# A hybrid decoder layer on one core: pools of the gate tiles and of the first FFN products moved, the second norm's root with priority, the down-projection's first tiles, and 1 KB of DMA scratch

## The chip, the cores and the metric

The kernel runs on one core of a Trainium2 chip. The metric is the device time of one execution in microseconds (us). The engines are TensorE (PE in the profile), VectorE (DVE), ScalarE (ACT), GpSimd (POOL) and SyncE (SP), whose queue issues the DMAs. Each engine works its own queue in order.

## The reference

One layer (DEPTH is 1) over 1040 tokens (16 meta tokens and 1024 of the input), model width 1024, all in float32:

```python
proj = h @ w_in
q_lat, kv_lat, k_pe, z, xbc, dt_raw, g_attn, g_ssd = split(proj)
y_attn = mla_branch(q_lat, kv_lat, k_pe, ...)
y_ssd = ssd_branch(z, xbc, dt_raw, ...)   # ends in: y * silu(z), rms norm per group, * norm_g, @ w_o_ssd
mixed = sigmoid(g_attn) * y_attn + sigmoid(g_ssd) * y_ssd
h = layer_norm(ALPHA * h + mixed @ w_out)
u = causal_dwconv3(h @ w_up)              # 1024 -> 2 x 2816
gate, val = split(u, 2)
h = layer_norm(ALPHA * h + (silu(gate) * val) @ w_down)
return h[:, 16:]
```

## The kernel before, in words

Tensors lie with features on the 128 partitions and tokens along the free dimension. Each float32 product is made of three matmuls: an operand is split into a rounded high part H (a cast on ScalarE) and a rest L (a subtraction on VectorE), `split` at L197, and high by high, low by high and high by low are summed in PSUM. A split activation tile is called a form. Weights come in raw (`wraw`, two buffers), are split into `wh` and `wl` by `load_w` (L143) and are used once.

The kernel is written in Tile: the program gives operations in an order with priorities (`tc.high_priority`), and a scheduler places each instruction on its engine's queue. Tiles come from pools. A pool opened with "right" takes its place from the other end of SBUF; pools opened later reuse the place of pools that were closed, and what is written to such a place waits until the last reader of the earlier tile is done.

The stages that the change touches:

- **SSD stage** (from L767): convolutions, the scan by groups of four head pairs, and eight gate products `gs_gate` (L793). A gate has three PSUM tiles; each goes through a tanh (L801) into a tile of pool "G" (three buffers) and is stored to `ts_d` (L802). The scan's output y is stored to `y_d` (L922), the norm factors of each group to `rr_d` (L811). Four of the eight gates stand at the end of the stage.
- **y stage**: pools "Dr" (temporaries), "Dy" (33 tiles) and "Dm" on the right. `load_y` (L967) loads rr and sixteen y tiles for one half of the tokens (three buffers `yl`), multiplies (L975) and makes sixteen forms. Beside it, `w_or` is loaded in sixteen pieces and summed on VectorE (L983 to L989). Then, for each half, eight products w_o_ssd, the merge with the gates, and eight products w_out with the residual and the sum of squares (L1023 to L1040).
- **Second norm** (L1041 to L1067): `inv_root` (L201) sums over partitions with ones (L209), takes the root on VectorE and spreads it over the partitions by five matmuls (L218). `normed` (L991) scales and shifts the eight tiles (L992 on VectorE, L993 on ScalarE) and stores them to `h1_d`. Then the left-hand sides of a seven-product scheme (Strassen, Winograd's form) are formed on VectorE: T2, T3, T1, B2, and T4 after a GpSimd subtraction (L1066). The forms lie in "F1" and "F2"; the temporaries in "Dr" and "Dz".
- **FFN up-projection** (L1069 to L1215): for each of 22 blocks f, up-projection weights a11, a12 and a21, a22 are loaded; GpSimd makes s1 to s4 from them (L1106 to L1109); five splits go into pool "E1" with six buffers of each kind. Products are numbered 1 to 7; each is 24 matmuls into half a PSUM pair (`prod`). The first four blocks (`NHEAD`) are treated apart: product 1 needs only B1, which is ready since the first norm, so it stands ahead (loop at L1157), its result copied to p1 (L1164), product 2 on top, copied to c11 (L1155). Then `first(f)`, product 6, and the main loop at L1170, which ends with the stores of gate times value to `gv_d`. E1 is opened after `eD.close()`, which closes "Dr" and "Dz".
- **Down-projection** (from L1219): the residual is loaded and scaled by `load_r` (L1250) and transposed into PSUM by PE (L1291), the activations come through `load_g` (L1241), split into `dh`, the weights through `load_d` (L1226); blocks of 4, 4, 4, 5 and 5 of the 22 rows (`KBLK`, L91) are worked over four token tiles. `norm2` (L1261) needs the gains g2 and b2, which GpSimd's queue loads (L1222, L1223).

## Time and profile before

| | |
|---|---|
| runs | 2530.03, 2522.92, 2524.55 us; median 2524.55 us |
| profiled execution | 2529.95 us, span 2527.8 us, mean granted TensorE clock 0.98 |
| busy | PE 96%, DVE 66%, ACT 44%, POOL 7% of the span |
| moved | 257.10 MB, 102 GB/s in the mean; 30.9% of the 16 DMA engines' time on the hardware queue |
| chain that ended last | PE 87%, DVE 6%, DMA 2% |

The profile is one execution, and its durations are summed against its own 2529.95 us. With PE busy for 96% of the span, the questions are where the rest stands and what PE waits for there. A window gives each engine's busy time in a stretch and the granted clock as a share of full speed (2.4 GHz; 0.50 is 1.2 GHz). A timeline gives an engine's instructions in order, with the idle time ahead of each and what ended it.

### The profile page before, as it was taken

Reading aid. Unit: us, or ns where it says so; the run is one execution under the profiler, and the core shown is the slowest. Engines: PE = TensorE matmul, PEld = TensorE weight load, DVE = VectorE, ACT = ScalarE, POOL = GpSimd, SP = SyncE. Lnnn points to the kernel's source line nnn. Section 1 sums busy time; section 2 is a strip of 40 time slices with the busy share of each in tenths; the row PEclk is TensorE's granted clock in tenths of the full one; section 3 lists DMA queues with packets and bytes.
Section 4 is the critical chain, followed back from the end, with each engine's and each line's share of the span. In section 5 each row is a group of like instructions: output and inputs, shape, how many; then the busy total and the mean of one; then the engine's idle time right before and its main releaser. Section 6 shows DMA issues by size and latency. Waiting matters only on the chain.

```text
span 2527.8 us, 42547 instructions
## 1 busy us (share of the span) xinstructions
PE 2422.2 (96%) x16451; PEld 2288.7 (91%) x16451; DVE 1664.3 (66%) x3834; ACT 1112.8 (44%) x2436; POOL 167.1 (7%) x170
## 2 busy tenths in 40 slices
PE   6999999999999999999999899999599999989998
PEld 6998998899999999999999889999589999988886
DVE  6467677674557777776777376745687777765624
ACT  5335455562245554555554233422535444455211
POOL 0000000000000000000000001001332222200000
PEclk9999999999999999999999999999799999999999
DMA  5121111152432222222121375544222222247432
GB/s 200 46 65 33 37 37 34 47 156 78 155 121 90 85 70 77 85 79 82 59 94 53 117 243 167 194 132 141 84 78 89 85 77 76 76 166 233 152 103 73
DMA packets 113530, 257.10 MB, mean 102 GB/s; under 512 B 13488, under 2 KB 48560, under 8 KB 111280
## 3 DMA queue, kind: packets, MB, share of 16 engines
q1 hardware_dynamic: 113040, 253.34, 30.9%
q8 instruction: 129, 2.11, 0.3%
q0 software_dynamic: 288, 1.05, 0.1%
q14 instruction: 73, 0.60, 0.1%
HBM read 200.97 MB, written 51.26 MB: 100 GB/s over the span
## 4 chain that ended last, share of the span: by engine, by line
PE 87%; DVE 6%; DMA 2%; ACT 1%; issue 1%; POOL 0%; SPq 0%; DVEq 0%; ACTq 0%; POOLq 0%
PE d L191 25%; PE g L171 12%; PE g L173 12%; PE g L172 12%; PE c L1300 9%; PE c L605 3%; PE c L878 2%; PE c L902 1%; PE c L599 1%; PE c L882 1%; DMA yl<-y_d 1%; DVE f L199 1%; PE c L552 1%; PE c L554 1%; PE c L556 1%
## 5 line engine op out<-in xcount | busy, mean ns | idle before, releaser
L191 PE MATMUL d<-f,wh 128*128 128x258 f32 (+1 forms) x4000 | 661.5, 288 | 45.8 <-ACT p L1164 16.0
L191 PEld LDWEIGHTS d<-f,wh 128*128 128x128 f32 x4000 | 564.9, 194 | 50.3 <-ACT p L1164 16.5
L171 PE MATMUL g<-h,wh 128*128 128x348 f32 (+3 forms) x1560 | 507.0, 325 | 4.7 <-ACT lat L387 4.7
L172 PE MATMUL g<-h,wl 128*128 128x348 f32 (+3 forms) x1560 | 507.6, 325 | 0.0
L173 PE MATMUL g<-h,wh 128*128 128x348 f32 (+3 forms) x1560 | 506.6, 325 | 0.0
L191 PE MATMUL d<-f,wl 128*128 128x258 f32 (+1 forms) x2000 | 408.8, 287 | 4.0 <-DVE wl L199 2.3
L191 PEld LDWEIGHTS d<-f,wl 128*128 128x128 f32 x2000 | 317.0, 195 | 5.3 <-DVE wl L199 2.9
L161 DVE TENSOR_TENSOR wl<-wraw,wh 128x512 fp32r<-128x512 f32 (+2 forms) x278 | 194.5, 701 | 179.9 <-ACT wh L160 176.6
L171 PEld LDWEIGHTS g<-h,wh 128*128 128x128 f32 x1560 | 294.9, 189 | 7.6 <-ACT lat L387 5.0
L172 PEld LDWEIGHTS g<-h,wl 128*128 128x128 f32 x1560 | 294.9, 189 | 2.5 <-issue 2.4
L173 PEld LDWEIGHTS g<-h,wh 128*128 128x128 f32 x1560 | 294.8, 189 | 2.4 <-issue 2.4
L160 ACT CAST wh<-wraw 128x512 fp32r<-128x512 f32 (+2 forms) x278 | 167.0, 604 | 250.7 <-PE g L173 124.5
L1300 PE MATMUL c<-wh,dh 128*128 128x512 f32 x704 | 193.3, 396 | 7.7 <-ACT dh L198 7.5
L198 ACT CAST wh<-wraw 128x512 fp32r<-128x512 f32 x154 | 90.9, 619 | 246.7 <-PE c L1300 97.6
L199 DVE TENSOR_TENSOR wl<-wraw,wh 128x512 fp32r<-128x512 f32 x154 | 102.9, 693 | 133.7 <-ACT wh L198 96.5
L1300 PEld LDWEIGHTS c<-wh,dh 128*128 128x128 f32 x704 | 133.0, 190 | 38.3 <-ACT dh L198 8.1
L171 PE MATMUL g<-a,wh 128*128 128x348 f32 (+2 forms) x456 | 149.5, 328 | 1.4 <-DVE kn L199 1.1
L173 PE MATMUL g<-a,wh 128*128 128x348 f32 (+2 forms) x456 | 148.2, 325 | 0.0
L172 PE MATMUL g<-a,wl 128*128 128x348 f32 (+2 forms) x456 | 147.9, 324 | 0.0
L783 DVE SCALAR_TENSOR_TENSOR xc<-g,V,xc 128x347 f32<-128x347 f32 (+2 forms) x180 | 103.6, 575 | 41.9 <-ACT xc L779 39.0
L868 ACT ACTIVATE G<-ac,tok 116x116 f32<-116x116 f32 x288 | 91.6, 379 | 42.6 <-PE c L878 42.6
L1300 PE MATMUL c<-wl,dh 128*128 128x512 f32 x352 | 110.1, 394 | 0.0
(270 smaller groups left out, 3883.9 us busy)
## 6 DMA issues: line engine op xcount, KB each, us to landing
wraw<-win SPq DMA_DIRECT2D x65, 512.0 KB, 3.4
wraw<-wup SPq DMA_DIRECT2D x48, 512.0 KB, 3.6
wraw<-wdl SPq DMA_DIRECT2D x44, 512.0 KB, 3.6
ac<-cs_d SPq DMA_DIRECT2D x16, 1044.0 KB, 5.6
wraw<-wos SPq DMA_DIRECT2D x32, 512.0 KB, 4.0
gv<-gv_d SPq DMA_DIRECT2D x44, 256.0 KB, 4.1
yl<-y_d SPq DMA_DIRECT2D x32, 257.0 KB, 3.8
wraw<-wout SPq DMA_DIRECT2D x16, 512.0 KB, 3.4
```

Source lines behind the costliest of these rows:

```text
L160: nc.scalar.copy(h[:, :n * ncol], r)
L161: nc.vector.tensor_sub(l[:, :n * ncol], r, f32(h[:, :n * ncol]))
L171: nc.tensor.matmul(ps, ah, bh, start=(k == 0), stop=False)
L172: nc.tensor.matmul(ps, al, bh, start=False, stop=False)
L173: nc.tensor.matmul(ps, ah, bl, start=False, stop=(k == n - 1))
L191: nc.tensor.matmul(ps[:, PO + c0:PO + c1], a, b[:, c0:c1], start=(start and k == 0 and i == 0), stop=(k == n - 1 and i == 2), skip_group_c ...
L198: nc.scalar.copy(H, src)
L199: nc.vector.tensor_sub(L, src, f32(H))
L605: nc.tensor.matmul(ops[:, o0:n], vt[j][:w, hh * P:(hh + 1) * P], ptt[:w, o0:n], start=(j == 0), stop=(j == nbmax - 1))
L783: nc.vector.scalar_tensor_tensor(t[:, l:n], ps[:, hal + l - s:hal + n - s], vec("cw", (3 - s) * 24 + ct), t[:, l:n], ALU.mult, ALU.add)
L868: nc.scalar.activation(G_[:, k * S:(k + 1) * S], ac[:S, hh, C0[b] + k * S:C0[b] + (k + 1) * S], AF.Relu, bias=tok[:, 3 * b + k, 32 + hd:33 ...
L1300: nc.tensor.matmul(pss[q], a, b, start=False, stop=(k == NFF - 1 and i == 2))
```

## The change

1. Pool "G" is opened on the left below "py", ahead of the o_proj stage, and closed after it; the right side is free during the SSD stage.
2. A pool "E0" is opened beside "F2", ahead of the second norm. It holds p1, c11, s1 to s4, and the splits for products 7, 6 and 3 (four buffers). "E1" comes after the first four blocks' products 1 and 2, and holds the splits for 5 and 4 (three buffers), u2, u4, ga, va and gb. The four b21 tiles are temporaries in "Dr" now, loaded late.
3. The second norm's `inv_root` has priority 400, the loop over the first four blocks 300 instead of 200. GpSimd's order is s1, s2, s3, s4. The condition that starts a block ahead has f + 1 instead of f + 2.
4. In the down-projection the blocks are 2, 4, 4, 4, 4, 4; `dh` of the first four rows has a pool of its own with 8 tiles; g2 and b2 go through SyncE's queue, and are placed after `norm2`.
5. The DMA scratch of the program is 1 KB.

```diff
-KBLK = ((0, 4), (4, 8), (8, 12), (12, 17), (17, 22))
+KBLK = ((0, 2), (2, 6), (6, 10), (10, 14), (14, 18), (18, 22))
...
     cut_psum(3)
+    eG = ctx.enter_context(ExitStack())
+    pgs = eG.enter_context(pool("G", 3))
     eY = ctx.enter_context(ExitStack())
     pyy = eY.enter_context(pool("py", 48))
...
-    with pool("G", 3, "right") as pgs, pool("C", 1) as p:
+    with pool("C", 1) as p:
...
     eY.close()
+    eG.close()
...
     eM.close()
     pf2 = eF.enter_context(pool("F2", 40))
-    pz = eD.enter_context(pool("Dz", 8, "right"))
-    rd = inv_root(ssq, HN, 1.0 / D, LN_EPS)
+    p0 = eF.enter_context(pool("E0", 1))
+    pz = eD.enter_context(pool("Dz", hB, "right"))
+    with tc.high_priority(400):
+        rd = inv_root(ssq, HN, 1.0 / D, LN_EPS)
...
-    b11, b21 = [], []
+    b11 = []
     for j in range(hB):
-        for b, k in ((b11, j), (b21, j + hB)):
-            b.append(ftile(pz, F32))
-            nc.sync.dma_start(b[-1], h1_d[k][:, cols(0)])
+        b11.append(ftile(pz, F32))
+        nc.sync.dma_start(b11[-1], h1_d[j][:, cols(0)])
...
     for j in range(hB):
-        nc.gpsimd.tensor_sub(b21[j], b21[j], t2[j])
-        T4[j] = form(pf2, b21[j])
-    eD.close()
-    pe = eF.enter_context(pool("E1", 1))
+        b21 = dtmp("b21", "r", 8)
+        nc.sync.dma_start(b21, h1_d[j + hB][:, cols(0)])
+        nc.gpsimd.tensor_sub(b21, b21, t2[j])
+        T4[j] = form(pf2, b21)
...
-            def stile(name):
-                return pe.tile([P, 512], F32, name=name, tag=name)
-
-            s1, s2, s3, s4 = (stile(k) for k in ("s1", "s2", "s3", "s4"))
-            nc.gpsimd.tensor_sub(s3, a11, a21)
+            s1, s2, s3, s4 = (p0.tile([P, 512], F32, name=k, tag=k) for k in ("s1", "s2", "s3", "s4"))
             nc.gpsimd.tensor_add(s1, a21, a22)
             nc.gpsimd.tensor_sub(s2, s1, a11)
+            nc.gpsimd.tensor_sub(s3, a11, a21)
             nc.gpsimd.tensor_sub(s4, a12, s2)
...
             for q, a in ((4, a22), (7, s3), (6, s2), (5, s1), (3, s4)):
-                r[q] = wsplit(pe, a, 6)
+                r[q] = wsplit(p0, a, 4) if q in (7, 6, 3) else wsplit(pe[0], a, 3)
...
-    def etile(name, bufs, n=HN):
-        return pe.tile([P, n], F32, name=name, tag=name, bufs=bufs)
+    pe = []
+
+    def etile(name, bufs):
+
+        return (p0 if name in ("p1", "c11") else pe[0]).tile([P, HN], F32, name=name, tag=name, bufs=bufs)
...
-        st[f]["c11"] = etile("ga", NHEAD + 1)
+        st[f]["c11"] = etile("c11", NHEAD)
...
-        with tc.high_priority(200):
+        with tc.high_priority(300):
...
+    eD.close()
+    pe.append(eF.enter_context(pool("E1", 1)))
     first(0)
...
-        ga = conv_up(c11, f, "ga", NHEAD + 1)
+        ga = conv_up(c11, f, "ga", 2)
...
-        while begun < min(NFF, f + (3 if f + 2 < NHEAD else 2)):
+        while begun < min(NFF, f + (3 if f + 1 < NHEAD else 2)):
...
-    with pool("Er", 8) as pr, pool("Eh", 50) as ph, pool("Ew", 1) as p:
-        g2 = p.tile([P, D], F32, name="g2")
-        b2 = p.tile([P, D], F32, name="b2")
-        nc.gpsimd.dma_start(g2, ln2[0:1].broadcast_to([P, D]))
-        nc.gpsimd.dma_start(b2, ln2[1:2].broadcast_to([P, D]))
+    with pool("Er", 8) as pr, pool("Eh0", 8) as ph0, pool("Eh", 44) as ph, pool("Ew", 1) as p:
...
-                H = ph.tile([P, 512], F32R, name="dh", tag="dh")
-                L = ph.tile([P, 512], F32R, name="dh", tag="dh")
+                H, L = ((ph0 if k < 4 else ph).tile([P, 512], F32R, name="dh", tag="dh") for _ in range(2))
...
+        g2 = p.tile([P, D], F32, name="g2")
+        b2 = p.tile([P, D], F32, name="b2")
+        nc.sync.dma_start(g2, ln2[0:1].broadcast_to([P, D]))
+        nc.sync.dma_start(b2, ln2[1:2].broadcast_to([P, D]))
         for r in range(2):
...
-    nc = _bacc.Bacc("TRN2", target_bir_lowering=False, num_devices=1)
+    nc = _bacc.Bacc("TRN2", target_bir_lowering=False, num_devices=1, dynamic_dma_scratch_size=1024)
```

The change moves instructions on several engines. In the rows below, the lines of the changed kernel are some three higher than before (L977 is the load of yl, L974 that of rr, L804 the store of a gate tile, L1168 the copy to p1, L1159 that to c11, L996 the norm's shift). A number behind a name tells tiles apart.

SyncE's queue at the end of the gates, before: the last gate's stores, then the first loads of rr and y.

```order
L802 DMA ts_d7_143<-ga_16884 128x334
L802 DMA ts_d7_143<-ga_16912 128x348
L802 DMA ts_d7_143<-ga_16940 128x344
L147 DMA wraw_17272<-wos 128x1024
L971 DMA rr_16963<-rr_d0_160 128x514
L974 DMA yl_16965<-y_d0_144 128x514
L974 DMA yl_16972<-y_d1_145 128x514
L974 DMA yl_16979<-y_d2_146 128x514
```

The same place in the changed kernel, at the stores of gate 5:

```order
L977 DMA yl_16986<-y_d3_147 128x514
L977 DMA yl_16995<-y_d4_148 128x514
L804 DMA ts_d5_141<-ga_16696 128x334
L977 DMA yl_17002<-y_d5_149 128x514
L974 DMA rr_17053<-rr_d3_163 128x514
L804 DMA ts_d5_141<-ga_16724 128x348
L977 DMA yl_17009<-y_d6_150 128x514
L977 DMA yl_17016<-y_d7_151 128x514
L977 DMA yl_17025<-y_d8_152 128x514
L804 DMA ts_d5_141<-ga_16752 128x344
L147 DMA wraw_17145<-wos 128x1024
L977 DMA yl_17032<-y_d9_153 128x514
```

The loads of y3 to y15 stand between the gate stores now; those of y0 to y2 stand in the SSD stage, and the sixteen loads of `wor` in the stage before.

PE at the second norm, before (d_20630 and d_20667 are product 1 of blocks 0 and 1):

```order
L209 MATMUL d_20448<-ones_74,ssq_19905 128x1 x5
L218 MATMUL d_20469<-K_73,ir_20455 128x128
L191 MATMUL d_20630<-f_18953,wh_20622 128x258
L191 MATMUL d_20667<-f_18953,wh_20659 128x258
L191 MATMUL d_20630<-f_18953,wh_20622 128x256
L191 MATMUL d_20667<-f_18953,wh_20659 128x256
```

and in the changed kernel (there d_20628 and d_20665):

```order
L209 MATMUL d_20451<-ones_74,ssq_19905 128x1 x5
L218 MATMUL d_20472<-K_73,ir_20458 128x128 x2
L218 MATMUL d_20472<-K_73,ir_20458 128x2
L218 MATMUL d_20472<-K_73,ir_20458 128x128 x2
L191 MATMUL d_20628<-f_18953,wh_20620 128x258
L191 MATMUL d_20665<-f_18953,wh_20657 128x258
L191 MATMUL d_20628<-f_18953,wh_20620 128x256
L191 MATMUL d_20665<-f_18953,wh_20657 128x256
```

Before, the other four L218 stand behind the 48 matmuls of these two products; now all five stand ahead of them.

ScalarE at the forms and the copies to p1, before (f_20596 to f_20611 are T4's):

```order
L198 CAST f_20596<-f_20477 128x514
L198 CAST f_20601<-f_20481 128x514
L198 CAST f_20606<-f_20485 128x514
L198 CAST f_20611<-f_20489 128x514
L198 CAST wh_20884<-wraw_20874 128x512
L1164 COPY p1_20655<-d_20630 128x514
L198 CAST wh_20888<-s3_20878 128x512
L198 CAST wh_20892<-s2_20877 128x512
L198 CAST wh_20896<-s1_20876 128x512
L198 CAST wh_20900<-s4_20879 128x512
L1164 COPY p1_20692<-d_20667 128x514
```

and in the changed kernel, first among the norm's shifts, then at the splits for products 7, 6 and 3 of block 0:

```order
L198 CAST f_20495<-t2_20493 128x514
L996 ACTIVATE r_20098<-r_20098,V_72 128x514
L198 CAST wh_20720<-wraw_20718 128x512
L198 CAST wh_20724<-wraw_20718 128x512
L1168 COPY p1_20653<-d_20628 128x514
L1168 COPY p1_20690<-d_20665 128x514
L198 CAST f_20508<-t2_20506 128x514
L996 ACTIVATE r_20366<-r_20366,V_72 128x514
L198 CAST f_20521<-t2_20519 128x514
L198 CAST wh_20783<-wraw_20781 128x512
L1168 COPY p1_20753<-d_20728 128x514
```

```order
L198 CAST wh_20891<-s3_20881 128x512
L198 CAST wh_20895<-s2_20880 128x512
L198 CAST wh_20903<-s4_20882 128x512
L1159 COPY c11_20716<-d_20628 128x514
L1159 COPY c11_20779<-d_20665 128x514
L1159 COPY c11_20842<-d_20728 128x514
L1159 COPY c11_20868<-d_20791 128x514
L198 CAST f_20574<-r_20232 128x514
L198 CAST f_20578<-r_20299 128x514
L198 CAST f_20582<-r_20366 128x514
```

The copies to p1 stood behind the last form; now three of them stand among the norm's shifts, and the copies to c11 stand behind the split of s4, ahead of the casts of B2 and T4.

## Rows read from the trace of the kernel before

**Rows 1.** The page: busy time, and PE by forty slices.
```profile
PE 2422.2 (96%) x16451; PEld 2288.7 (91%) x16451; DVE 1664.3 (66%) x3834; ACT 1112.8 (44%) x2436; POOL 167.1 (7%) x170
...
PE   6999999999999999999999899999599999989998
```

**Rows 2.** Windows; columns: stretch, length, each engine's busy time (count), clock, DMA, GB/s.
```profile
1443.90:1500.00 56.10, 42.62 (x290) 40.27 (x290) 42.51 (x68) 18.23 (x31) 0.00 (x0) 0.85 0.84 268
1500.00:1510.00 10.00, 10.00 (x85) 10.00 (x84) 4.56 (x7) 3.12 (x5) 0.00 (x0) 1.00 0.60 194
690.00:720.00 30.00, 30.00 (x192) 29.80 (x192) 10.60 (x21) 6.45 (x13) 0.24 (x3) 1.00 0.41 131
```

**Rows 3.** PE timeline, gates to w_o_ssd; columns: start, busy, engine, line, what [idle before].
```profile
1443.60 0.32 PE L173 MATMUL g<-h,wh 128*128 128x344 f32 x1
1453.06 0.80 PE L191 MATMUL d<-f,wh 128*128 128x258 f32 x2 [9.14 <-ACT f L198]
```

**Rows 4.** SyncE timeline, same place: DMA issues.
```profile
1425.64 8.38 SPq L802 DMA_DIRECT2D ts_d<-ga  x3
...
1436.90 8.38 SPq L802 DMA_DIRECT2D ts_d<-ga  x3
...
1445.85 0.39 SPq L971 DMA_DIRECT2D rr<-rr_d  x1
```

**Rows 5.** Windows, second norm to FFN, and the FFN loop.
```profile
1754.96:1900.00 145.04, 106.66 (x774) 104.33 (x774) 103.84 (x150) 62.38 (x102) 41.08 (x28) 0.84 0.25 80
1900.00:2200.00 300.00, 300.00 (x2488) 300.00 (x2487) 222.69 (x298) 144.70 (x237) 80.67 (x60) 1.00 0.25 78
```

**Rows 6.** PE timeline, 1750 to 1800.
```profile
1757.23 1.25 PE L209 MATMUL d<-ones,ssq 128*128 128x1 f32 x10 [2.27 <-DVE ssq L1039]
1760.90 0.76 PE L218 MATMUL d<-K,ir 128*128 128x128 f32 x2 [2.42 <-DVE ir L230]
...
1769.31 1.05 PE L218 MATMUL d<-K,ir 128*128 128x128 f32 x8
...
1783.36 0.77 PE L191 MATMUL d<-f,wh 128*128 128x258 f32 x2 [9.62 <-ACT r L993]
...
1799.46 0.80 PE L191 MATMUL d<-f,wh 128*128 128x258 f32 x2 [11.54 <-ACT p L1164]
```

**Rows 7.** ScalarE timeline, forms and p1.
```profile
1794.27 2.18 ACT L198 CAST f<-f 128x514 fp32r<-128x514 f32 x4
...
1798.82 0.58 ACT L1164 COPY p<-d 128x514 f32<-128x514 f32 x1
```

**Rows 8.** PE timeline, start of the down-projection.
```profile
2269.06 2.07 PE L1300 MATMUL c<-wh,dh 128*128 128x512 f32 x4 [7.54 <-ACT dh L198]
```

**Rows 9.** ScalarE timeline, same place.
```profile
2267.19 1.26 ACT L1257 ACTIVATE hr<-hr 128x512 f32<-128x512 f32 x2 [0.37 <-DMA hr<-h_d]
```

**Rows 10.** Groups on DVE, 1450 to 1500: line, what, shapes, count | busy, mean | idle before.
```profile
L975 DVE SCALAR_TENSOR_TENSOR yl<-yl,half_sg,rr 128x514 f32<-128x514 f32 x16 | 11.8, 752 | 9.6 <-DMA yl<-y_d 9.5
L199 DVE TENSOR_TENSOR f<-yl,f 128x514 fp32r<-128x514 f32 x16 | 11.0, 687 | 0.2
L987 DVE TENSOR_REDUCE wm<-wr 128x1 f32<-128x512 f32 x16 | 10.6, 678 | 0.0
```

**Rows 11.** DVE timeline, second norm.
```profile
1771.30 2.06 DVE L992 SCALAR_TENSOR_TENSOR r<-r,V,d 128x514 f32<-128x514 f32 x3
...
1781.82 1.40 DVE L992 SCALAR_TENSOR_TENSOR r<-r,V,d 128x514 f32<-128x514 f32 x2
...
1785.60 2.39 DVE L1059 TENSOR_TENSOR r<-r 128x514 f32<-128x514 f32 x2
```

**Rows 12.** The page's DMA issues: count, KB each, median us to landing.
```profile
wraw<-wup SPq DMA_DIRECT2D x48, 512.0 KB, 3.6
```

**Rows 13.** GpSimd timeline, second norm.
```profile
1785.81 1.63 POOL L1066 TENSOR_TENSOR f<-f,t 128x514 f32<-128x514 f32 x1 [2.50 <-issue]
1798.95 2.26 POOL L1106 TENSOR_TENSOR s<-wraw 128x512 f32<-128x512 f32 x1 [11.51 <-DVE f L199]
```

## The prediction

> **What bounds the kernel now.** The page comes first: TensorE (PE) is busy 96% of the 2527.8 us span, and its row of forty slices falls below 9 only at the start, in a few slices in the middle and at the end [rows 1]. So only time in which PE stands still, or runs at half clock, can be won. I then looked for the stretches where it does, with the windows, and read in each the PE timeline for the wait and the queue of the engine named as releaser. Three such stretches lie where the diff works.
>
> **Stretch A, from the last gate product to the first products of w_o_ssd (1443.9 to 1500).** 290 matmuls ran in 56.1 us; the ten us behind show the full rate, 85 in 10 us [rows 2]. At that rate 290 take 34.1 us, so 22.0 us are lost. The timeline shows the largest piece: the last gate matmul ends at 1443.92, the next starts at 1453.06 after 9.14 us, released by ScalarE's cast of a form [rows 3]; the rest is smaller waits and the lower clock behind that wait (0.85 granted over the whole stretch [rows 2]). The cause stands in SyncE's queue: the loads of rr and yl are issued at 1445.85 and not before, behind the stores of the last three gate tiles [rows 4]. Those y tiles lie on the right side of SBUF where the gate tiles "G" stood.
>
> **Stretch B, from the second norm into the first FFN products (1754.96 to 1900).** 774 matmuls in 145.04 us; the 300 us behind ran 2488 in 300 us, 0.1206 us each [rows 5]. 774 of them are 93.3 us: 51.7 us lost. The PE timeline names the pieces [rows 6]: 2.27 and 2.42 us around the root; the other four broadcasts of the root (L218) at 1769.31, 8 us after the first, behind 48 matmuls; 9.62 us released by L993 of the norm; 11.54 us released by the copy to p1 (L1164), and smaller ones. That copy needs a tile of pool E1, which opens only when Dz, Dr and their tiles are closed, that is, after the T4 forms: the copy runs at 1798.82, right behind the last casts of forms [rows 7].
>
> **Stretch C, into the down-projection.** PE waits 7.54 us before 2269.06 for the first cast of dh [rows 8], which stands on ScalarE right behind two scalings of hr that end at 2268.45 [rows 9].
>
> **The change, part by part: A.** With "G" on the left the y stage's right-hand tiles wait for nothing of the gates. By the order, the loads of y0 to y2 go into the SSD stage, y3 to y15 between the last nine gate stores, and the sixteen sums of w_or go back into the o_proj and gate stage, where DVE is busy 10.60 of 30 us [rows 2]: the 16 by 0.678 us = 10.8 us [rows 10] are hidden there. Thirteen forms remain to be made during the gates. One costs DVE 0.752 + 0.687 us [rows 10], 18.7 us in all, against nine gate tiles at a third of the 11.26 us from the stores of one gate to those of the next (1425.64 to 1436.90 [rows 4]), about 34 us. If they were late by two or three us it would still cost nothing, since the first product takes the sixteen forms one after another over 96 matmuls, 11.3 us. What is left is the tanh that frees the last gate's PSUM, about 1.1 us (estimate: a cast that stands ahead of it and itself, each near a cast's 0.55 us [rows 7]). The new place has a price: SyncE now waits in the SSD stage for stores of y and rr to land, six or seven times, with weight loads queued behind it. The raw weights are two buffers ahead, and PE was never short there; I take 0 and keep 5 us as the bad end. **A: 22.0 - 1.1 = 20.9 us gained, bounds 15 and 22.**
>
> **B.** The root with priority puts all five L218 together, so the norm starts when the first two did, some 8 us earlier (1761.7 instead of 1770.4 [rows 6]). Pool E0 holds p1, c11 and s1 to s4 beside F2 from the start, so the p1 copies wait for no form. The second products (x0 with q 2) and f3's first then run during the norm. What still is lost, on the clock of before:
> - ssq, root and broadcasts, unchanged: 1754.96 to 1760.90 less little work, 5.9 us.
> - f3's first product takes the PSUM pair that rd holds, so it waits for the eighth L992. Before, these took from 1771.30 to 1783.22 [rows 11], 11.9 us; from 1763.2, and with four weight splits and p1 copies put between, that is 1776.9. PE has 72 matmuls until then, to about 1773: 4 us.
> - The seconds last until about 1789.6. f0's product 6 then waits for c11, which stands on ScalarE behind the split of s4. Its raw load can be issued when f3's low half is split, about 1782.5, lands 3.6 us later [rows 12], five POOL instructions of 1.3 us end at 1793.0, two ScalarE ones at 1794.3: 4.7 us.
> - Product 5 needs the split of s1, which stands behind three c11 copies, eight casts of forms (four took 2.18 us [rows 7]) and another split: about 1803.3 against 1798.4 for PE: 5 us.
> - f1's and f2's splits of s2 come late by 3 and 1.5 us.
> - PE starts at half clock after each longer wait, four times. Such a start took 8.0 us for 48 matmuls between 1761.31 and 1769.31 [rows 6], against 5.8: 2.2 us, so 8.8 in all.
>
> Together 5.9 + 4 + 4.7 + 5 + 4.5 + 8.8 = 32.9 us. **B: 51.7 - 32.9 = 18.8 us gained.** The bounds: if every wait is 50% longer and the clock falls once more, 8 us; if the queues overlap as well as they can and only the root, f3's wait and two half-clock starts stay (14 to 20 us), 32 us. I take the value in the middle, since each step has its own row.
>
> **C.** The 1 MB of g2 and b2 leaves the time of the first gv loads, and one hr scaling fewer stands between the last store and dh; the gv loads still stand behind the same stores. Lower bound 0; upper 3 us, somewhat under half of the 7.54. I take 1.5, about one scaling (0.63) and a landing shorter by one us. The smaller first block needs only two gv tiles for its first 48 matmuls, which hid nothing before: PE showed no wait after 2269.06. The scratch size only makes room.
>
> **Nothing.** The loop from f = 4 on ran without a gap, 300.00 of 300 us [rows 5]. Its five splits had six buffers of each kind and now have four and three, which is one to spare in each pool; by the order each split stands at least 140 matmuls, some 17 us, ahead of its product. I cost it at 0; the cover is that distance.
>
> **Sum.** 20.9 + 18.8 + 1.5 = 41.2 us. The profiled execution took 2529.95 us and would take 2488.8. The median of the runs shown is 2524.55, 5.4 lower; taking the same 41 us off gives **2483.5 us**.
>
> **The rivals.**
> 1. *VectorE and GpSimd hold each other up.* Beside a GpSimd subtraction of 1.63 us [rows 13] two VectorE subtractions took 2.39 us, where two instructions of the same size just before took 1.40 [rows 11]. After the change four more GpSimd instructions (s1 to s4 of f0) fall among the forms, and each would add its length to VectorE's chain: 4 by 1.3 to 1.6 us, some 6 us, passed on to the waits for s1 and for f1's weights. GpSimd in turn would wait for VectorE: the first sum that ran beside a form took 2.26 us [rows 13]. With both B gains 10, the total is 32: 2492. For: the rows. Against: part of it is already in the forms' times. Chance 0.15.
>    The Trainium skill, "SBUF — State Buffer", section "SBUF: two separate sides", says that the port pair of the two engines is an exclusive lock, held for the whole instruction, against a VectorE operation with two inputs in SBUF. By that rule the forms' subtractions would be blocked in full, and the trace agrees in the pair of rows just named.
> 2. *B's waits only move.* The chain raw load, GpSimd, ScalarE for f0 to f2 is late by as much as the p1 copies were, so B gains 4: 26 us in all, 2498. For: GpSimd still starts its sums only after the raw load. Against: some 96 matmuls more are done by then. Chance 0.12.
> 3. *B hides nearly all*, 30 us: 52 us, 2472. For: three of the waits reckoned above hang on ScalarE's in-order queue, where one that ends earlier lets all behind it pass. Chance 0.11.
> 4. *Slower: the narrow weight pools in the loop.* If a split in E1 (three buffers) waits for its slot until the product of the f before is done, PE stalls once in each of the 18 iterations from f = 4. At 2.3 us each (cast, subtraction and a wait between engines: 0.6 + 0.7 + about 1) that is 41 us and eats the gain; slower than before by over 0.3% takes 2.7 us each, at 3.5 us it would be 2546. Against: the 17 us of distance. Chance 0.04.
> 5. *It doesn't do what it says*: the scheduled order shows the moves, so only if waits at run time hold them back to the same end. Within 0.3%. Chance 0.03.
>
> **How the numbers follow.** My own case has 0.55. It lies between 2477 and 2490. The range takes the bounds of A, B and C: 15 + 8 + 0 = 23 gives 2501.5, 22 + 32 + 3 = 57 gives 2467.5; so 2467 to 2502, which holds rivals 1 to 3 and leaves out 4 and 5 and the odd miss beyond the bounds. About 0.3%, 7.6 us, is what a measurement can tell from no change. Faster by more: 0.55 + 0.15 + 0.12 + 0.11 = 0.93, of which I move 0.01 to no change for what I have not seen: 0.92; within: 0.04; slower: 0.04.
>
> **What would show it.** A right: no wait over 2 us on PE between the gates and w_o_ssd, yl loads among the gate stores on SyncE, clock 1.00 there. B right: L218 five times in one row, p1 copies among the norm's instructions, then two waits of about 5 us near c11 and the split of s1. C right: a wait of about 6 instead of 7.5 us before the first down-projection matmul. Wrong, if PE has gaps between 1900 and 2200 of the old clock, if the SSD stage is longer by over 5 us, or if the second norm's stretch still loses over 45 us.

## The result and the profile after

The changed kernel takes 2496.43 us (median of 4 runs, 2494.66 to 2499.16) against 2524.91 us (4 runs, 2522.92 to 2530.03): 28.5 us less, a ratio of 0.9885 with a 95% interval from 0.9868 to 0.9902. The forecast was 2483.5 us in a range from 2467 to 2502: the right side and inside the range, but 13 us better than what came.

Where the time went is read by cutting the span at five points of the PE timeline: the end of the last gate matmul, of the last w_out matmul, of the last FFN product, the start of the first down-projection matmul and the end. Each stretch is the difference of two such times.

| kernel | A: gates to second norm | B: second norm and FFN products | C: to the down-projection | D: down-projection |
|---|---|---|---|---|
| before | 311.0 | 501.3 | 12.8 | 258.7 |
| changed | 294.0 | 490.5 | 12.2 | 260.4 |
| e1: G on the left alone | 291.5 | 500.5 | 12.6 | 258.3 |
| e2: changed, G on the right | 307.5 | 488.5 | 11.4 | 259.1 |
| e3: root's priority alone | 311.2 | 495.7 | 12.5 | 259.0 |
| e4: changed, old blocks | 295.5 | 488.9 | 12.0 | 258.1 |
| e5: changed, b21 on VectorE | 291.8 | 488.0 | 11.4 | 259.3 |
| e6: changed, product 4's split in E0 | 291.7 | 514.9 | 10.8 | 259.6 |
| e7: changed, c11 first | 294.1 | 489.0 | 12.6 | 258.0 |
| e8: changed, y15's cast on VectorE | 290.9 | 489.5 | 12.1 | 262.0 |
| e9: changed, no priority for the root | 294.3 | 495.4 | 10.9 | 260.9 |
| e10: changed, no forms of B2 and T4 | 295.8 | 483.8 | 12.1 | 259.3 |
| e11: b21 and y15 on VectorE | 290.0 | 485.9 | 12.5 | 259.9 |
| e12: e10 with three raw buffers | 292.3 | 479.9 | 11.4 | 258.3 |

Each row is one profiled execution, and unchanged code differs by 1 to 4 us between rows, so a difference of one or two in one cell says nothing by itself: with the changed kernel's code there, A is 291.7 to 295.8 and B 488.5 to 490.5. Before against changed, A gives 17.0, B 10.8, C 0.6 and D -1.6; the remaining 3.8 of the 30.6 us between the two spans lie ahead of A. They can't be put down to the change: the gates end at 1439 to 1444 in all these runs, at 1443.9 before and at 1440.7 in e3, which has the old code there.

The page of the changed kernel, the same two lines as before [rows 1]:

```profile
PE 2412.9 (97%) x16451; PEld 2279.8 (91%) x16451; DVE 1675.0 (67%) x3834; ACT 1111.7 (45%) x2436; POOL 168.5 (7%) x168
...
PE   6999999999999999999999999999789999989998
```

The dip at the gates is gone, that at the second norm is shallower (a 5 before, now a 7 and an 8). The PE timeline, at the four places of [rows 3, 6, 8]:

```profile
1443.28 0.50 PE L191 MATMUL d<-f,wh 128*128 128x258 f32 x2 [3.11 <-ACT ga L803]
...
1736.47 1.25 PE L209 MATMUL d<-ones,ssq 128*128 128x1 f32 x10 [2.27 <-DVE ssq L1042]
1740.15 2.47 PE L218 MATMUL d<-K,ir 128*128 128x128 f32 x10 [2.43 <-DVE ir L230]
...
1774.58 0.80 PE L191 MATMUL d<-f,wh 128*128 128x258 f32 x2 [5.78 <-ACT c L1159]
...
1783.10 0.77 PE L191 MATMUL d<-f,wh 128*128 128x258 f32 x2 [3.19 <-DVE u L1147]
...
2236.82 2.07 PE L1305 MATMUL c<-wh,dh 128*128 128x512 f32 x4 [8.45 <-ACT dh L198]
```

The 9.14 us behind the gates became 3.11. The five L218 stand in one row (ten records, 2.47 us). The waits for L993 and for p1, 9.62 and 11.54 us, are gone; in their place stand 5.78 us for c11 and 3.19 us. The down-projection waits as before: 8.45 us here, 7.54 in the kernel before, 7.08 to 8.88 in the other runs. The windows of the changed kernel (columns as in [rows 2, 5]):

```profile
1440.17:1500.00 59.83, 56.72 (x470) 56.73 (x471) 23.73 (x35) 16.70 (x28) 0.00 (x0) 1.00 0.44 145
...
1734.20:1742.27 8.07, 3.37 (x21) 3.35 (x21) 3.98 (x15) 1.25 (x2) 0.00 (x0) 0.77 0.22 65
1742.27:1750.33 8.06, 7.42 (x51) 7.22 (x50) 7.10 (x12) 4.69 (x8) 0.00 (x0) 0.80 0.45 166
1750.33:1768.80 18.47, 17.97 (x144) 17.54 (x144) 15.56 (x25) 11.57 (x21) 4.34 (x3) 1.00 0.46 157
1768.80:1774.58 5.78, 0.00 (x1) 0.01 (x1) 3.13 (x3) 2.40 (x5) 5.78 (x6) 0.84 0.03 9
1774.58:1790.08 15.50, 11.19 (x49) 10.42 (x49) 11.60 (x18) 10.93 (x19) 5.91 (x6) 0.62 0.19 65
1790.08:1854.52 64.44, 54.10 (x416) 52.24 (x417) 52.30 (x67) 25.64 (x41) 20.95 (x15) 0.97 0.26 87
1854.52:1880.00 25.48, 25.42 (x196) 25.21 (x197) 21.65 (x26) 11.22 (x18) 10.54 (x8) 0.93 0.22 73
1880.00:2180.00 300.00, 300.00 (x2487) 300.00 (x2485) 229.75 (x298) 145.77 (x237) 78.67 (x58) 1.00 0.25 80
```

From 1880 on PE is full again at 2487 matmuls in 300 us. Taking 0.1206 us per matmul off the stretches ahead of that gives what each lost: 8.1 for the root (its small matmuls counted as lost), 1.9 for the start at a granted 0.80, 1.1, 5.8, 9.6 at a granted 0.62, 14.3 between 1790 and 1854, and 1.8.

The same can be counted in both kernels, since PE runs the same number of these matmuls in every run: 192 of the first four blocks' products 1 and 2, then as many as block 0 has left (120), as blocks 1 to 3 have (360) and as block 4 has (168). They are counted in order of time, so a product of the next block that runs early is counted with the block ahead. These are the windows of the 360 before and in the changed kernel (two of the 362 matmuls reach in from ahead):

```profile
1835.27:1890.27 55.00, 48.71 (x362) 47.71 (x361) 44.25 (x59) 20.23 (x32) 17.11 (x12) 0.91 0.27 87
```

```profile
1800.66:1858.02 57.36, 48.27 (x362) 46.83 (x361) 48.58 (x62) 23.85 (x37) 18.21 (x13) 0.94 0.26 84
```

At 0.1206 us each, 360 matmuls take 43.4 us. What each part of B lost, counted in this way:

| lost, us | before | changed | e5 | e10 | e12 |
|---|---|---|---|---|---|
| root, to the first product | 6.4 | 8.1 | 8.1 | 8.1 | 8.1 |
| the 192, and the wait behind them | 34.3 | 9.2 | 6.2 | 7.3 | 6.8 |
| block 0's 120 | 2.0 | 11.6 | 11.6 | 9.3 | 9.3 |
| the 360 of blocks 1 to 3 | 11.6 | 13.9 | 14.3 | 10.1 | 8.6 |
| block 4's 168 | 0.0 | 0.4 | 0.8 | 1.9 | 0.0 |

In e2, e4 and e8, whose code in B is the changed kernel's, the second line is 8.3 to 9.0, the third 11.4 to 12.0 and the fourth 11.4 to 13.5. So of the 25 us won at the 192 block 0 gives ten back, and blocks 1 to 3 lose at least what they lost before, within the scatter of these runs.

### The profile page after: what moved, and what is told of

Read it like the earlier page. It is cut to its first block, busy times and chain, and to the rows that moved or that the text cites. A ratio compares the mean times of both kernels' runs of the same rounds, so it can differ in the third digit from the quotient of the medians.

```text
span 2497.2 us, 42526 instructions
## 1 busy us (share of the span) xinstructions
PE 2412.9 (97%) x16451; PEld 2279.8 (91%) x16451; DVE 1675.0 (67%) x3834; ACT 1111.7 (45%) x2436; POOL 168.5 (7%) x168
## 4 chain that ended last, share of the span: by engine, by line
PE 83%; DVE 7%; DMA 4%; ACT 2%; issue 1%; POOL 1%; SPq 0%; DVEq 0%; ACTq 0%; POOLq 0%
PE d L191 24%; PE g L171 12%; PE g L173 12%; PE g L172 12%; PE c L1305 7%; PE c L605 3%; PE c L880 2%; PE c L904 1%; PE c L599 1%; PE c L884 1%; DMA yl<-y_d 1%; DMA gv<-gv_d 1%; DVE f L199 1%; PE c L552 1%; PE c L554 1%
## 5 line engine op out<-in xcount | busy, mean ns | idle before, releaser
L172 PEld LDWEIGHTS g<-h,wl 128*128 128x128 f32 x1560 | 294.3, 189 | 2.5 <-issue 2.4
L199 DVE TENSOR_TENSOR wl<-wraw,wh 128x512 fp32r<-128x512 f32 x154 | 111.5, 750 | 150.6 <-ACT wh L198 106.6
```

The costliest lines, as they stand in the source:

```text
L172: nc.tensor.matmul(ps, al, bh, start=False, stop=False)
L199: nc.vector.tensor_sub(L, src, f32(H))
```

## The experiments

A ratio in brackets, with its 95% interval, is to the kernel before, timed anew beside each group of runs; its median there was 2523.66 to 2525.30 us. Differences to the changed kernel are to its 2496.43 us, from another group, so one or two us of such a difference say little.

### e1, e2: the gate tiles' pool

The pools of the o_proj stage need the place of the larger scratch once G stands on the left, so the two go together (the runs don't take them apart, but e2 keeps the scratch), and e1 is the kernel before with

```diff
+    eG = ctx.enter_context(ExitStack())
+    pgs = eG.enter_context(pool("G", 3))
     eY = ctx.enter_context(ExitStack())
-    with pool("G", 3, "right") as pgs, pool("C", 1) as p:
+    with pool("C", 1) as p:
+    eG.close()
-        nc.gpsimd.dma_start(g2, ln2[0:1].broadcast_to([P, D]))
+        nc.sync.dma_start(g2, ln2[0:1].broadcast_to([P, D]))
...
+    ..., dynamic_dma_scratch_size=1024)
```

and e2 the changed kernel with the pool's lines undone (the scratch and the loads of g2 and b2 kept).

> The kernel before with pool G on the left, the 1 KB scratch (without which the pools of the o_proj stage don't fit) and, since the scratch belongs to GpSimd's DMAs, g2 and b2 loaded by SyncE at their old place. Theory (the parts add up): the changed kernel's trace shows 17 us less between the last gate product and the second norm, so 2524.9 - 17 = 2508 us, and the second norm's stretch loses its 51.7 us as before. Rival (the y loads only displace other waits, which come back later in the stretch or in the SSD stage): 2515 us or more.

> The changed kernel with pool G back on the right. Theory: the 17 us come back, 2496.4 + 17 = 2513 us, the 9 us of PE idle time before w_o_ssd stand in the trace again. Rival (other parts of the change cover some of it): 2505 us or less.

e1 took 2507.91 us, 17.0 less than before (ratio 0.9934, 0.9918 to 0.9951); e2 took 2514.31, 17.9 more than the changed kernel (0.9956 against before, 0.9939 to 0.9973). The first wait of PE behind the gates in each (PE timeline):

```profile
1445.67 0.51 PE L191 MATMUL d<-f,wh 128*128 128x258 f32 x2 [2.58 <-ACT ga L803]
```

```profile
1449.39 0.80 PE L191 MATMUL d<-f,wh 128*128 128x258 f32 x2 [9.13 <-ACT f L198]
```

The place of G makes the 9 us wait, and nothing else in the change covers it. The waits on stores that came into the SSD stage cost nothing that shows: e1's gates end at 1443.1, those of before at 1443.9, and those of e3, with the old order, at 1440.7.

### e3, e9: the root's priority

e3 is the kernel before with the priority alone; e9 the changed kernel without it.

```diff
-    rd = inv_root(ssq, HN, 1.0 / D, LN_EPS)
+    with tc.high_priority(400):
+        rd = inv_root(ssq, HN, 1.0 / D, LN_EPS)
```

> The kernel before with the priority on the second norm's root and nothing else: the five L218 stand together, p1 still waits for the T4 forms. Theory (the priority carries most of the gain at the second norm, because the forms and so the p1 copies end some 8 us earlier): 2524.9 - 8 = 2517 us. Rival (pool E0 carries it: without it the first GpSimd sums, the weights' split and the p1 copies wait for something else than the forms): within 3 us of before, 2522 to 2525.

> The changed kernel without the priority on the second norm's root, so that four of the five L218 stand behind the products 1 of blocks 0 and 1 again. The priority alone took 5.6 us off the stretch from the second norm to the end of the FFN products in the kernel before, all parts together 10.8. Theory (the two add up): the stretch loses 5 to 6 us, 2501.5 to 2502.5 us. Rival (with E0 the p1 copies don't hang on the forms, so the later forms are hidden): 2499 or less.

e3: 2518.68 us, 6.2 less than before (0.9977, 0.9966 to 0.9988). e9: 2503.37 us, 6.9 more than the changed kernel (0.9907, 0.9892 to 0.9922). Both are within 2 us of their theories and away from their rivals. B is 5.6 us shorter in e3, 4.9 longer in e9. e3's PE timeline and ScalarE's copy to p1 in it:

```profile
1758.48 2.47 PE L218 MATMUL d<-K,ir 128*128 128x128 f32 x10 [2.42 <-DVE ir L230]
...
1791.44 0.80 PE L191 MATMUL d<-f,wh 128*128 128x258 f32 x2 [11.69 <-ACT p L1165]
```

```profile
1790.81 0.58 ACT L1165 COPY p<-d 128x514 f32<-128x514 f32 x1
```

The p1 wait is as long as before (11.69 against 11.54), but the whole chain of forms ends earlier: the copy starts at 1790.81 instead of 1798.82, of which 3.0 us come from the earlier start of the stretch and 5.0 from the priority. That is less than the 8 us between the first and the later L218 of before, in part since all five take 2.47 us here. So the two parts add up: about 5 us of B belong to the priority, about 5 to the rest of the change there, that is, E0 with the new orders and the loop's priority, which no run takes apart.

### e4: the blocks of the down-projection

```diff
-KBLK = ((0, 2), (2, 6), (6, 10), (10, 14), (14, 18), (18, 22))
+KBLK = ((0, 4), (4, 8), (8, 12), (12, 17), (17, 22))
```

> The changed kernel with the old blocks of the down-projection (4, 4, 4, 5, 5). From the first down-projection matmul to the end the changed kernel took 260.4 us where the kernel before took 258.7, with a new wait of 0.95 us on a weight split and a lower clock behind it. Theory (the new blocks put casts of dh that wait for gv loads ahead of that split): the wait goes, 1 to 2 us less, 2494.5 to 2495.5, with 258.7 in the trace. Rival (g2 and b2 on SyncE's queue hold the weight loads up): the wait stays, 2496.

2496.77 us, as the changed kernel: the rival's time. The wait did go, as the theory had it: behind its first wait PE has none in D, where the changed kernel has 0.95 us at 2297.99; of the ten profiles with the new blocks six have such a wait (0.73 to 1.57 us), of the four with the old ones none. But D is 258.1 here, and e7, which has the new blocks, has 258.0, e8 262.0. Over all profiles the new blocks have 258.0 to 262.0 and the old ones 258.1 to 259.0: 1.2 us on average against the new blocks (259.7 of ten, 258.5 of four), too little for the times to show.

### e5: GpSimd beside VectorE

```diff
-        nc.gpsimd.tensor_sub(b21, b21, t2[j])
+        nc.vector.tensor_sub(b21, b21, t2[j])
```

> The changed kernel with the four b21 subtractions on VectorE instead of GpSimd. In the changed kernel's trace GpSimd's first sum takes 3.11 us beside a run of form subtractions, one b21 stands between s2 and s4 (1.72 us), and product 6 waits 5.78 us for c11 behind the split of s4. Theory (the price of the two engines beside each other is a few tenths of each instruction, and only the b21 ahead of s4 counts): s4 ends 1.5 us earlier, VectorE gets 2.8 us more work, in sum -2 to +1 us: 2494.5 to 2497.5. Rival 1 of the prediction (GpSimd and VectorE holding each other up is what the missing 8 us of the second norm's stretch went to): 4 us or more less, 2492 or below.

2493.01 us (0.9871, 0.9854 to 0.9887): 3.4 less than the changed kernel, between the two expectations. B is 2.4 less than in the changed kernel and 0.5 to 1.5 less than in e2, e4 and e8; e11, with the same edit here, has 485.9. GpSimd's first sums in the changed kernel and here:

```profile
1764.46 3.11 POOL L1107 TENSOR_TENSOR s<-wraw 128x512 f32<-128x512 f32 x1 [45.58 <-DMA wraw<-wup]
1767.53 1.29 POOL L1109 TENSOR_TENSOR s<-wraw 128x512 f32<-128x512 f32 x1
1768.78 1.26 POOL L1108 TENSOR_TENSOR s<-s,wraw 128x512 f32<-128x512 f32 x1
1770.00 1.72 POOL L1072 TENSOR_TENSOR b<-b,t 128x514 f32<-128x514 f32 x1
1771.68 1.70 POOL L1110 TENSOR_TENSOR s<-wraw,s 128x512 f32<-128x512 f32 x1
```

```profile
1761.68 1.44 POOL L1107 TENSOR_TENSOR s<-wraw 128x512 f32<-128x512 f32 x1 [45.18 <-DMA wraw<-wup]
1763.08 1.75 POOL L1109 TENSOR_TENSOR s<-wraw 128x512 f32<-128x512 f32 x1
1764.80 1.73 POOL L1108 TENSOR_TENSOR s<-s,wraw 128x512 f32<-128x512 f32 x1
1766.61 1.59 POOL L1110 TENSOR_TENSOR s<-wraw,s 128x512 f32<-128x512 f32 x1
```

From the start of the first sum to the start of s4 it was 7.22 us and is 4.93: one b21 less (1.72); the first sum is 1.67 shorter, but the next two are 0.93 longer together. PE's wait for c11 went from 5.78 to 3.22, and the one behind it from 3.19 to 3.91; blocks 1 to 3 lose as much as in the changed kernel (14.3 and 13.9). The shorter first sum isn't the edit's doing: e4, whose code here is the changed kernel's, has 1.48, 1.74 and 1.74 for the three, and a wait of 4.91 for c11. So what the edit surely saves is b21's place in GpSimd's queue. The two engines' mutual delay remains in e5, and no run shows what it costs alone.

### e6: which split lies in which pool

```diff
-            for q, a in ((4, a22), (7, s3), (6, s2), (5, s1), (3, s4)):
-                r[q] = wsplit(p0, a, 4) if q in (7, 6, 3) else wsplit(pe[0], a, 3)
+            for q, a in ((7, s3), (6, s2), (4, a22), (5, s1), (3, s4)):
+                r[q] = wsplit(p0, a, 4) if q in (7, 6, 4) else wsplit(pe[0], a, 3)
```

> The changed kernel with the split for product 4 (of the raw half a22) in E0 and that for product 3 in E1, so that a22 is split ahead of the forms of B2 and T4. Theory (the missing 8 us stand in blocks 1 to 3: their second raw load waits for the buffer that a22 of the block before holds, and that split waits for its place in E1, which is free only behind the last forms; the load was issued at 1783.58 where the first stood at 1773.41): block 1's second load is issued some 8 us earlier, the small waits of blocks 1 to 3, some 11 us of idle time and low clock, fall by half: 2496.4 - 5 = 2491.5 us. Rival (these waits come from GpSimd's four sums per block and ScalarE's queue, whatever the load does): within 2 us, 2494.5 to 2498.

2523.80 us (0.9993, 0.9982 to 1.0004): both expectations missed, by 26 us or more. The load did move: block 1's two raw loads are issued at 1773.38 together (SyncE's timeline, against 1773.41 and 1783.58 in the changed kernel). But the loop, which had no gap, now has small ones, 11.7 us in 300 (windows, and ScalarE's waits from 1900 to 2200, in e6 and then in the changed kernel: what waited for what, us in total, times, longest):

```profile
1900.00:2200.00 300.00, 288.33 (x2324) 283.58 (x2325) 199.38 (x276) 132.15 (x221) 82.33 (x56) 0.99 0.21 73
```

```profile
ACT wh L198 <- DMA wraw<-wup: 96.6, 14, 8.1
```

```profile
ACT wh L198 <- DMA wraw<-wup: 41.8, 14, 4.0
```

ScalarE's queue waits 96.6 us of 300 for loads instead of 41.8, with the copies that free PSUM behind it, and 2324 matmuls run where 2487 did. B is 24.4 us longer, 1.4 us for each of 18 blocks: this is the fourth rival of the prediction in a version two lines away. The likely reason is that product 4 is a block's last: with its split in the pool of four a raw half stays in its buffer longer, and the next load comes later. But the edit changes the order of the splits together with their pools, so which of the two did it is not shown.

### e7: c11 ahead of the splits

```diff
-        nc.scalar.copy(st[f]["c11"], half(st[f]["x0"]))
+        with tc.high_priority(600):
+            nc.scalar.copy(st[f]["c11"], half(st[f]["x0"]))
```

> The changed kernel with a higher priority for the copies to c11, which puts three of them ahead of the splits of s2 and s4 on ScalarE. Theory (PE's 5.78 us before product 6 are half ScalarE's order: c11 is copied only behind the split of s4, 3.3 us after that of s2): product 6 then starts behind the split of s2, the wait is 2.5 to 3 us shorter, and of this 1 to 3 us reach the end: 2493.5 to 2495.5. Rival (the next wait, for product 5, takes it all back, since it hangs on the casts of the forms): 2496 to 2497.5.

2498.41 us (2495.80 to 2501.82): no gain, and B, at 489.0, is that of e2, e4 and e8. In the PE timeline the 5.78 us fall apart, and the next wait grows:

```profile
1769.75 0.50 PE L191 MATMUL d<-f,wh 128*128 128x258 f32 x2 [1.35 <-ACT wh L198]
1772.73 0.79 PE L191 MATMUL d<-f,wl 128*128 128x258 f32 x2 [2.48 <-DVE wl L199]
...
1782.14 0.77 PE L191 MATMUL d<-f,wh 128*128 128x258 f32 x2 [4.33 <-DVE u L1147]
```

1.35 and 2.48 us for the split of s2, then 4.33 where there were 3.19: product 5 takes most of it back, as the rival said.

### e8: the last tanh

```diff
+                if hi == 0 and ti == 15:
+                    H, L = ftile(pyh), ftile(pyh)
+                    nc.vector.tensor_copy(H, yt)
+                    nc.vector.tensor_sub(L, yt, f32(H))
...
```

> The changed kernel with the cast of the last y form (y15, first half) on VectorE instead of ScalarE. In the changed kernel's trace PE waits 2.3 to 3.6 us behind the last gate product for the last tanh, where the prediction had 1.1, and on ScalarE that tanh and the one before stand behind the cast of y15, whose load landed last. Theory (ScalarE's order makes it): the wait falls to 1 to 1.5 us, 2494 to 2496 us. Rival (the tanh waits for its tile, that is, for the store of an earlier gate tile on SyncE): the wait stays over 2 us, 2496 to 2497.

2497.02 us (2493.50 to 2499.08), no difference in the times; the trace answers. ScalarE at the last gate of the changed kernel, and PE's first wait in e8:

```profile
1440.86 0.62 ACT L198 CAST f<-yl 128x514 fp32r<-128x514 f32 x1 [3.29 <-DVE yl L978]
1441.39 0.45 ACT L803 ACTIVATE ga<-g 128x348 f32<-128x348 f32 x1
...
1442.77 0.46 ACT L803 ACTIVATE ga<-g 128x344 f32<-128x344 f32 x1
```

```profile
1443.81 0.50 PE L191 MATMUL d<-f,wh 128*128 128x258 f32 x2 [1.07 <-ACT ga L803]
```

In the changed kernel a tanh of gate 7 waited behind the cast of y15 (3.29 us for VectorE's product, that is, for the load), and the last one behind that and two casts of a weight. Without the cast the wait is the 1.07 us of the prediction, and 1.07 again in e11, which has the same edit; in all the other runs with G on the left it is 2.10 to 3.57. A is 3.1 us shorter in e8 and 4.0 in e11, where unchanged code differs by 4; in e8 D is 1.6 longer than in the changed kernel.

### e10, e12: the late forms and the raw buffers

e10 leaves work out, so its result is not the layer's:

```diff
-    for j in range(hB):
-        B2[j] = form(pf2, rs[j + hB])
-    for j in range(hB):
-        b21 = dtmp("b21", "r", 8)
-        nc.sync.dma_start(b21, h1_d[j + hB][:, cols(0)])
-        nc.gpsimd.tensor_sub(b21, b21, t2[j])
-        T4[j] = form(pf2, b21)
+    B2, T4 = T1, T2
```

> The changed kernel without the forms of B2 and T4 (their products read T1's and T2's forms instead, so that eight casts, eight subtractions and the four b21 loads and subtractions are left out). Theory (the missing 8 us of the second norm's stretch hang on these forms: E1's place is free only behind them, so the splits for products 5 and 4 of block 0 come late, with them the raw buffer and the load of block 1): product 5's wait goes (3 us and the low clock behind it), block 1's second load is issued some 8 us earlier, and the stretch loses 6 to 9 us less: 2487.5 to 2490.5 us. Rival (GpSimd's sums and two raw buffers bound blocks 1 to 3 whatever the forms do): 2 to 4 us less, as without the b21 subtractions on GpSimd, 2492.5 to 2494.5.

2489.72 us (2488.66 to 2491.99), 6.7 less than the changed kernel; B is 6.7 less, and 4.7 to 5.7 less than in e2, e4 and e8, whose code in B is the changed kernel's. Of it some 2.4 are the b21 subtractions (e5), so the forms of B2 and T4 hold PE up by some 2 to 4 us; whether by their casts or by their subtractions no run tells. PE's waits and block 1's raw loads (SyncE):

```profile
1773.54 0.80 PE L191 MATMUL d<-f,wh 128*128 128x258 f32 x2 [4.12 <-ACT c L1153]
...
1782.99 1.22 PE L191 MATMUL d<-f,wh 128*128 128x258 f32 x4 [5.00 <-ACT wh L198]
```

```profile
1772.38 1.48 SPq L1085 DMA_DIRECT2D wraw<-wup  x2
```

The loads go out together, as forecast, but product 5's wait didn't go: 5.00 us, for the next thing in line. e12 adds a third raw buffer (`bufs=3` at the three places of `wraw`), in the place of the sixteen form tiles:

> As the kernel without the late forms (eight casts, eight subtractions, the b21 loads and subtractions left out), with a third buffer for raw weights, which the place of the sixteen form tiles makes room for. There PE still waits 5.00 us before product 5 of block 0 and 6 us in six small waits in blocks 1 to 3. Theory (two raw buffers bound these blocks: each block needs two loads, and the second waits until a half of the block before is split): the stretch from the second norm to the end of the FFN products loses 3 to 5 us less, 479 to 481 us of 483.8, and the whole 2485 to 2487 us. Rival (one set of s1 to s4 and ScalarE's queue bound them): the stretch stays within 1.5 us, the whole 2488 to 2491 us.

2487.66 us (2484.34 to 2491.34); the median is 2.1 below e10, and the ranges overlap. B is 479.9, 3.9 less, as the theory had it (the whole lies 0.7 above its range), but the profile of e12 is of its fastest execution and that of e10 of its slowest, so 3.9 may be too much. GpSimd's sums of blocks 0 and 1 in e12:

```profile
1753.83 1.29 POOL L1102 TENSOR_TENSOR s<-wraw 128x512 f32<-128x512 f32 x1 [40.85 <-DMA wraw<-wup]
...
1776.36 1.66 POOL L1102 TENSOR_TENSOR s<-wraw 128x512 f32<-128x512 f32 x1 [7.22 <-DVE wl L200]
```

Block 0's sums start 11.2 us earlier than in e10 (1753.83 against 1765.00; 2.2 of it come from the earlier start of the stretch), since the raw load no longer waits for a buffer. The next bound shows at once: block 1's s1 waits 7.22 us for the split of block 0's s1, of which there is one tile. A second set of s tiles wasn't tried, so that this is what holds blocks 1 to 3 now is not shown.

### e11: a version that beats both

> The changed kernel with the b21 subtractions and the cast of y15 on VectorE, as the version that may beat both kernels. Theory (the two act in different stretches and add up): 2493.0 less 1 to 2 us, 2491 to 2492 us. Rival (the second is hidden by the first products' waits on weights): 2493.

With both edits, e5's and e8's: 2491.92 us (2489.02 to 2492.81; 0.9873, 0.9858 to 0.9887), 31.7 less than the kernel before beside it (2523.66) and 4.5 less than the changed kernel (2494.66 to 2499.16); 1.1 less than e5 alone, as much as the expectation and less than the scatter.

## Why the prediction was right, and where it was not

The time fell as forecast and lies in the range, but the range was 35 us wide and the forecast 13 us too good: A's mechanism held, B won little more than half of its sum.

- **The three stretches, and that only PE's idle time counts**: right. A, B and C are where the time came from, and the loop from f = 4 on stayed full (2487 in 300 us). Most of the signs came: the y loads among the gate stores, clock 1.00 behind the gates, five L218 in one row, copies to p1 among the norm's shifts (from 1750.70), and a wait of 5.78 for c11. Three did not: PE's wait at the gates is over 2 us, the second wait named is 3.19, for `u2` on VectorE, instead of 5 for a split of s1, and C's wait is 8.45 us, not about 6.
- **A, 20.9 us forecast, 17.0 measured**, 17.0 and 17.9 by the times of the two runs with the pool alone, within the bounds of 15 and 22. The mechanism and the hidden price of the moved sums held. The term that was too small is "what is left is the tanh ... about 1.1 us": it was 3.11, because the y loads now end with the gates, and the last cast of a form stands ahead of the tanh on ScalarE. That is 2.0 of the missing 3.9 us. Another 0.9 was never there: at B's 0.1206 us a matmul the stretch to 1500 had lost 21.1 us, not 22.0, since the 85 in 10 us count matmuls that the window's ends cut. The rest is within A's scatter. I had costed the thirteen forms by VectorE's busy time and said that a delay of two or three us would cost nothing since the first product takes the forms one after another. True for PE, but not for what stands behind the waiting cast on its own engine (e8).
- **B, 18.8 us forecast, 10.8 measured** (11.8 to 12.8 in e2, e4 and e8). By its own list: the root 5.9 forecast, 8.1 measured, since the four L218 moved ahead weigh on PE there (2.47 us for ten records against 0.76 for two) and I had costed them at nothing; f3's wait of 4 us did not come, which made up for part of the miss by luck (VectorE ended the eighth L995 at 1754.96, where the forecast 1776.9, less the 20.8 us by which the stretch began earlier, is 1756.1, and of the 119 matmuls that had started before f3's copy to p1 at 1759.76 some 23 were second products); c11 4.7, measured 5.8, and PE ran dry at 1768.8, which is the forecast 1789.6 less the same 20.8 us; product 5 and the low clock around it 9.4 (4.4 and 5), measured 9.6.

  **The step that failed** is the term for blocks 1 to 3, "f1's and f2's splits of s2 come late by 3 and 1.5 us": they lost 13.9 us (14.3 in the window from 1790 to 1854), not 4.5. The table of losses shows how it was mis-sized. Of the 51.7 us that the stretch lost before, 11.6 stood in these 360 matmuls, among the "smaller ones" of the prediction's list. By charging 4.5 for them the sum counted on some 7 us that nothing in the change wins, and that is most of the 8 missing. I had followed the chain of block 0 to its end, and only guessed that the next blocks' chains catch up with PE. What holds them is shown in part. Without the late forms the 360 lose 10.1 (e10), with a third raw buffer as well 8.6 (e12), against 11.4 to 13.9 in the runs with the changed kernel's code; the last 8.6 stay open. b21 on GpSimd has no part in it (14.3 in e5): its 2.4 us of B stand in the wait for c11.
- **C, 1.5 us forecast, 0.6 measured**, which can't be told from scatter, and the wait that was to be shorter is not; D was taken as 0, and the runs show some 1.2 us against on average, less than the 4 us by which D differs between runs with the same code.
- **The rivals.** The first (VectorE and GpSimd) gave 2492, the second (waits only move) 2498; the time lies between. The second is seen at work: block 0's 120 matmuls lost 2.0 us before and 11.6 after. The first is seen in single instructions, but its share of the time is not. The fourth, slower, is what e6 showed, 24.4 us in B, with a different choice of the splits. That the "17 us of distance" protects the loop held for the change as written, but it says little of what a small edit does.

## What to carry to other kernels

When a stall is removed at the start of a stage with a pipeline behind it, follow the second and third turn of that pipeline as closely as the first, and read what they lose already before the change: which buffer holds the next load back, which cast frees it, and what stands ahead of that cast on its in-order engine. A wait that PE can absorb is not free if its instruction stands ahead of another that PE needs. And before tiles change their pools, ask which of them is used last in a turn, since its place comes free last; that is the likely reason why e6 lost nearly all of the gain.

## What the runs showed of the hardware that I had not expected

VectorE and GpSimd can delay each other more evenly than I had taken it from [rows 11, 13]. In e12 the four sums of block 0 ran while VectorE had work of its own; VectorE's timeline of that moment:

```profile
1754.00 1.67 DVE L200 TENSOR_TENSOR wl<-wraw,wh 128x512 fp32r<-128x512 f32 x1 [0.38 <-ACT wh L199]
1755.59 1.77 DVE L200 TENSOR_TENSOR f<-t,f 128x514 fp32r<-128x514 f32 x1
1757.29 1.78 DVE L1059 TENSOR_TENSOR f<-r,f 128x514 f32<-128x514 f32 x1
1758.99 1.78 DVE L1064 TENSOR_TENSOR r<-r 128x514 f32<-128x514 f32 x1
```

Four subtractions of the kind that takes 0.69 us (in e5, at 1756.95) took 1.67 to 1.78 each, one to each GpSimd sum (which started at 1753.83, 1755.08, 1756.78 and 1758.59 and took 1.29, 1.74, 1.74 and 1.63): the two engines took turns, and both lost. The Trainium skill ("SBUF — State Buffer", section "SBUF: two separate sides") calls the port pair of the two an exclusive lock that is held for a whole instruction; this alternation, at some 1.7 us for a pair, agrees with it.

They don't always take turns. Here is the same run of four subtractions on VectorE, beside GpSimd's first sums, in the changed kernel and in e4, which has the same code there:

```profile
1763.92 2.50 DVE L199 TENSOR_TENSOR f<-f 128x514 fp32r<-128x514 f32 x4
```

```profile
1764.32 5.79 DVE L199 TENSOR_TENSOR f<-f 128x514 fp32r<-128x514 f32 x4
```

In the changed kernel the first sum started 0.54 us into the run, took 3.11 us and ended 1.15 us behind it. VectorE lost nothing (four such subtractions took 2.49 at 1779.86, with GpSimd idle), and the second and third sum took 1.29 and 1.26. In e4 it started 0.35 us into the run and took 1.48, the next two 1.74 each, and VectorE's run took more than twice as long. So an overlap of the two engines can fall out either way in the same kernel; what decides it is not shown.
